# An encoder block in float32: the last normalization read from PSUM, residuals added two tiles at a time, and other first instructions

## The chip, the core and the metric

The kernel runs on one core of a Trainium2 chip. The core has five engines that run side by side, each from a queue of its own, strictly in order: TensorE (PE, matrix products; PEld is its weight load), VectorE (DVE), ScalarE (ACT), GpSimd (POOL) and SyncE (SP, which here only starts transfers). PE writes only to PSUM, eight banks of 128 x 512 float32; DVE and ACT read PSUM and SBUF; POOL works on SBUF alone. Transfers (DMA) go between HBM and SBUF and are started from the queues of SP, ACT and POOL.

The metric is the device time of one execution in microseconds (us).

## The reference: what is computed

One residual layer over 512 tokens of width 2048. The change touches its first product, its row sums of squares and its very last step, so these are shown; attention, convolution and gating lie between.

```python
def rms_norm(x, g):
    xf = x.astype(jnp.float32)
    y = xf * lax.rsqrt(jnp.mean(xf * xf, axis=-1, keepdims=True) + EPS) * g.astype(jnp.float32)
    return y.astype(x.dtype)
...
u = rms_norm(h, mix_pre_g[l])
proj = u @ w_in[l]
...
u = rms_norm(h, ffn_pre_g[l])
gate, up = jnp.split(u @ w_gate_up[l], 2, axis=-1)
f = (jax.nn.silu(gate) * up) @ w_down[l]
h = h + rms_norm(f, ffn_post_g[l])
```

## The kernel before

Everything is held transposed: 16 tiles of 128 features by 512 tokens (KT = 16). Tokens fall into halves `A` (columns 0 to 255) and `B` (256 to 511). A float32 product is made of three fast ones: each operand is split into a rounded part (`hi`, a cast on ACT, line 124) and the rest (`lo`, a subtraction on DVE, line 125), and PE adds hi·lo, hi·hi and lo·hi (lines 170, 173, 174 in `gemm`; 185, 187, 188 in `interleaved`). `wchunk` loads 1024 columns of weights from SP's queue and splits them.

A scheduler puts the instructions of each engine into one fixed order when the program is built, from program order and priorities; `keep_in_program_order` pins an instruction's place, and `high_priority(offset=-TAIL)` shifts the priority of what is inside by 200. At run time each engine takes its queue in that order and waits for semaphores at the head of it.

**The start** (lines 92 to 106 and 388 to 395). POOL makes an identity matrix, a tile of ones and `mhalf`, four columns of -0.5. PE runs WARM = 24 transposes of the identity, whose results nobody reads. ACT starts the transfers of `vec` (the gains) and of the second half of the first x tiles. `follow` pins the first ACT cast and the first product behind this. Then, for eight steps of two x tiles, ACT makes `u..h` (x times gain, line 137), DVE makes `u..l` (line 138), ACT squares x (line 325), DVE adds the squares up (line 328), and PE multiplies into four banks. The first weight chunk is split in two halves of 512 columns.

**A row's rms** (`rstd`, lines 277 to 295, and `by_column`). PE multiplies the tiles of squares by a column of ones: one 128x1 product per tile of squares and block of 128 tokens, into one column of a PSUM tile per block (`r.._s`). DVE scales that and adds EPS (line 292), POOL raises it to -0.5 (line 294), and PE spreads the result over 128 partitions (line 301, `r.._b`, in PSUM). For the last norm, `halves` has ACT copy that to SBUF (line 319, `r4`).

**The end** (lines 754 to 829). The w_down products run in two passes over the hidden dimension. In the second, DVE adds each result to `y` (line 772), ACT squares it, and ACT multiplies `y` by the post gain in place (line 774). The last two of the 16 features' tiles, 14 and 15, are computed by `products` for the token half A first and then for B, so that the work on half A's norm can lie beside the products of half B (`pl`, banks `pl1_14` and `pl1_15`). `first_half` then runs `finish` for 16 tiles of half A: y·r4 (line 794) and + h (line 795), on POOL for every third tile and on DVE otherwise, and SP starts one transfer out per tile (line 820). After the products of half B, DVE adds their results (line 786), ACT squares them (line 787), and the rms of half B, 16 more `finish` and five transfers out (line 829) end the kernel.

## Time and profile before

| | us |
|---|---|
| median of 3 runs (lowest, highest) | 2588.96 (2587.96, 2590.28) |
| the profiled execution | 2587.58 |
| its span, first to last instruction | 2585.8 |
| PE, DVE, ACT, POOL busy | 2535.4, 1751.2, 1079.6, 263.9 |
| mean granted TensorE clock | 0.991 of full |

The 1.8 us between the profiled execution's time and its span lie around the program. PE is busy for 98% of the span, so what can be saved lies in places where PE waits, and at the two ends, where the other engines work alone. Times in the rows below count from the span's start. In a group's row stand line, engine, operation, tiles written and read, the count, and then minimum, median and maximum of one instruction in nanoseconds or, in the rows by time, start and duration in us and the wait before it in brackets.

### The profile page before, as it was taken

The numbers are of one execution on the slowest core, as the hardware profiler recorded it, in microseconds if no ns is written. First come the engines' busy times: TensorE is split into PE (matmuls) and PEld (weight loads), VectorE is DVE, ScalarE is ACT, GpSimd is POOL, SyncE is SP. The second block draws the span as 40 slices with busy tenths as digits, with TensorE's granted clock in tenths as the row PEclk, the third lists the DMA queues.
The fourth block names the chain that finished last, engine by engine and source line by source line (L and its number), as shares of the span: only waits on it lengthen the run. The fifth ranks groups of instructions, "written<-read, shape, count | busy, mean of one in ns | idle before, by whom it ended". The sixth has DMA issues, their size and how long they took to land.

```text
span 2585.8 us, 33614 instructions
## 1 busy us (share of the span) xinstructions
PE 2535.4 (98%) x13078; PEld 2168.7 (84%) x13078; DVE 1751.2 (68%) x2224; ACT 1079.6 (42%) x1560; POOL 263.9 (10%) x290
## 2 busy tenths in 40 slices
PE   9999999989999999998999999999999999999996
PEld 8888888778888888887998888888888878888886
DVE  5999896687776655338888888888788832233336
ACT  5223333455554422224555555555555532233222
POOL 0110222320000011004100000000000100010003
PEclk9999999989999999999999999999999999999998
DMA  6234323356667435234356656656655653353334
GB/s 215 93 127 148 108 95 104 109 149 189 184 189 251 143 129 189 95 104 151 107 158 182 173 172 180 179 171 173 185 169 168 206 174 103 94 170 98 96 97 136
DMA packets 124624, 385.42 MB, mean 149 GB/s; under 512 B 14256, under 2 KB 21552, under 8 KB 124464
## 3 DMA queue, kind: packets, MB, share of 16 engines
q1 hardware_dynamic: 96464, 311.47, 37.0%
q0 software_dynamic: 13024, 45.62, 8.7%
q10 hardware_dynamic: 14976, 26.19, 2.8%
q8 instruction: 102, 1.67, 0.3%
q14 instruction: 58, 0.48, 0.1%
HBM read 350.72 MB, written 32.51 MB: 148 GB/s over the span
## 4 chain that ended last, share of the span: by engine, by line
PE 92%; DVE 4%; issue 2%; ACT 1%; DMA 1%; POOL 1%; POOLq 0%; DVEq 0%; ACTq 0%; SPq 0%
PE f L237 19%; PE f L239 10%; PE g L237 7%; PE pd L170 5%; PE pd L173 5%; PE pd L174 5%; PE g L239 3%; PE po L173 2%; PE po L174 2%; PE po L170 2%; PE qk L174 2%; PE qk L173 2%; PE qk L170 2%; PE py L170 2%; PE py L174 2%; PE py L173 2%
## 5 line engine op out<-in xcount | busy, mean ns | idle before, releaser
L125 DVE TENSOR_TENSOR wlo_wd<-raw_wd,whi_wd 128x1024 fp32r<-128x1024 f32 (+1 forms) x90 | 102.3, 1136 | 283.7 <-ACT whi_wd L124 283.7
L124 ACT CAST whi_wd<-raw_wd 128x1024 fp32r<-128x1024 f32 (+1 forms) x90 | 88.4, 982 | 312.8 <-PE pd L173 306.8
L376 DVE SCALAR_TENSOR_TENSOR cv<-z,vec,cv 128x497 f32<-128x497 f32 (+14 forms) x240 | 190.9, 797 | 4.7
L125 DVE TENSOR_TENSOR wlo_wo<-raw_wo,whi_wo 128x1024 fp32r<-128x1024 f32 x36 | 47.4, 1318 | 106.9 <-ACT whi_wo L124 106.9
L124 ACT CAST whi_wo<-raw_wo 128x1024 fp32r<-128x1024 f32 x36 | 37.9, 1054 | 130.0 <-PE po L173 122.7
L124 ACT CAST whi_y<-raw_y 128x1024 fp32r<-128x1024 f32 x32 | 33.5, 1052 | 78.8 <-PE py L173 75.5
L124 ACT CAST whi_qk<-raw_qk 128x1024 fp32r<-128x1024 f32 x32 | 33.6, 1051 | 77.1 <-PE qk L173 52.7
L125 DVE TENSOR_TENSOR wlo_qk<-raw_qk,whi_qk 128x1024 fp32r<-128x1024 f32 x32 | 40.4, 1261 | 32.3 <-ACT whi_qk L124 32.1
L125 DVE TENSOR_TENSOR wlo_y<-raw_y,whi_y 128x1024 fp32r<-128x1024 f32 x32 | 52.2, 1634 | 10.7 <-ACT whi_y L124 9.5
L616 DVE TENSOR_TENSOR gg<-py,gg 128x512 f32<-128x512 f32 x32 | 21.8, 690 | 53.1 <-PE py L174 53.1
L294 POOL TENSOR_TENSOR r_r<-r_v,mhalf 128x2 f32<-128x2 f32 (+1 forms) x6 | 7.7, 1283 | 458.2 <-DVE r_v L292 458.2
L735 POOL DMA_DIRECT2D ad<-a_d x44 | 24.0, 555 | 262.4 <-PE pd L170 197.6
L170 PE MATMUL py<-ycl,whi_y 128*128 128x512 f32 x128 | 49.8, 389 | 0.0
L173 PE MATMUL py<-ych,whi_y 128*128 128x512 f32 x128 | 49.8, 389 | 0.0
L174 PE MATMUL py<-ych,wlo_y 128*128 128x512 f32 x128 | 49.8, 389 | 0.0
L747 ACT ACTIVATE sg<-sg 128x512 f32<-128x512 f32 x39 | 24.7, 634 | 50.2 <-DVE sg L275 50.2
L455 POOL TENSOR_TENSOR bm<-braw,msk 128x128 f32<-128x128 f32 x56 | 43.0, 801 | 14.0 <-DMA braw<-in_rpb 13.9
L153 PE MATMUL f<-b,whi_f 128*128 128x256 f32 x128 | 36.2, 283 | 0.0
L154 PE MATMUL f<-b,wlo_f 128*128 128x256 f32 x128 | 36.2, 283 | 0.0
L152 PE MATMUL f<-b,whi_f 128*128 128x256 f32 x128 | 36.2, 283 | 0.0
L626 POOL TENSOR_TENSOR gg<-gg,gg 128x512 f32<-128x512 f32 x16 | 21.7, 1355 | 111.2 <-ACT whi_y L124 69.6
L124 ACT CAST whi_ca<-raw_ca 128x1024 fp32r<-128x1024 f32 x12 | 12.6, 1053 | 47.2 <-PE cb L173 19.0
(3045 smaller groups left out, 8284.4 us busy)
## 6 DMA issues: line engine op xcount, KB each, us to landing
raw_wd<-in_w_dn SPq DMA_DIRECT2D x60, 512.0 KB, 3.5
raw_wo<-in_w_out SPq DMA_DIRECT2D x36, 512.0 KB, 3.8
raw_qk<-in_w_qk SPq DMA_DIRECT2D x32, 512.0 KB, 3.7
raw_wd<-in_w_dn SPq DMA_DIRECT2D x30, 384.0 KB, 3.1
a_d<-sg ACTq DMA_DIRECT2D x44, 256.0 KB, 3.7
ad<-a_d POOLq DMA_DIRECT2D x44, 256.0 KB, 4.8
raw_v<-in_w_v SPq DMA_DIRECT2D x16, 512.0 KB, 4.4
raw_y<-in_w_ao SPq DMA_DIRECT2D x16, 512.0 KB, 3.7
```

What stands on the lines that cost most here:

```text
L124: nc.scalar.copy(hi[:, s], raw[:, s])
L125: nc.vector.tensor_tensor(out=lo[:, s], in0=raw[:, s], in1=hi[:, s].bitcast(F32), op=ALU.subtract)
L152: nc.tensor.matmul(o, hi, t[:, B], start=first, stop=False, skip_group_check=True)
L153: nc.tensor.matmul(o, hi, t[:, A], start=False, stop=False, skip_group_check=True)
L154: nc.tensor.matmul(o, lo, t[:, A], start=False, stop=last, skip_group_check=True)
L170: mmul = nc.tensor.matmul(ps, hi[:, s], al, start=first, stop=False)
L173: nc.tensor.matmul(ps, hi[:, s], ah, start=False, stop=False)
L174: nc.tensor.matmul(ps, lo[:, s], ah, start=False, stop=last)
L237: nc.tensor.matmul(ps, hi[:, ws[k]], t, start=first and k == 0, stop=False, skip_group_check=True)
L239: nc.tensor.matmul(ps[:, A], lo[:, ws[k]], t[:, A], start=False, stop=last and k == HT - 1, skip_group_check=True)
L376: nc.vector.scalar_tensor_tensor(out=a[:, to], in0=z[:, fr], scalar=col(C_WDW, i * CW + w), in1=a[:, to], op0=ALU.mult, op1=ALU.add)
L455: nc.gpsimd.tensor_tensor(out=bm[:, o + i - i0], in0=raw[:, :, i * BC : (i + 1) * BC], in1=msk[:, o + i - i0, None, :].broadcast_to([P, RO ...
```

## The change

- **Start.** `mhalf` is no longer set by POOL but computed by ACT from `ones`, pinned in its place: ACT's table load and this small instruction now stand ahead of the transfer of the second half of the first x tiles. The small `warm` instruction on ACT goes. PE's transposes become 17. The two halves of the first weight chunk are cast by DVE instead of ACT.
- **`rstd`** goes over the tiles of squares outside and over the token blocks inside, and only the very first product of a PSUM tile carries the start flag.
- **End.** The gain is no longer multiplied by ACT. `normalized` multiplies y by the gain and by 1/rms in one DVE instruction, which reads 1/rms straight from PSUM (`r.._b`); the copy `r4` goes. In half A the residual is added per tile, on DVE for every fourth tile and on POOL for twelve. In half B it is added for two tiles at once (128x512), on POOL for two of the eight pairs, and there are eight transfers out of two tiles each.

```diff
-WARM = 24
+WARM = 17
...
-    nc.gpsimd.memset(mhalf, -0.5)
-    warm = const.tile([P, 1], F32, name="warm")
-
+    tc.keep_in_program_order(nc.scalar.activation(mhalf, ones[:, :NB], AF.Copy, scale=-0.5))
     pw = abank("warm")
-    nc.scalar.activation(warm, mhalf[:, 0:1], AF.Square)
...
-    def wchunk(src, name, parts=1):
+    def wchunk(src, name, parts=1, cast=nc.scalar.copy):
...
-            nc.scalar.copy(hi[:, s], raw[:, s])
+            cast(hi[:, s], raw[:, s])
...
-        hi, lo = wchunk(w_c0[c], f"c0_{c}", 1 if c else 2)
+        hi, lo = wchunk(w_c0[c], f"c0_{c}", *((1,) if c else (2, nc.vector.tensor_copy)))
...
-        for t in blocks:
-            for i, a in enumerate(acc):
+        for i, a in enumerate(acc):
+            for t in blocks:
                 mmul = nc.tensor.matmul(
-                    ps[:, t : t + 1], a[:, t * P : (t + 1) * P], ones[:, 0:1], start=i == 0, stop=i == len(acc) - 1
+                    ps[:, t : t + 1], a[:, t * P : (t + 1) * P], ones[:, 0:1],
+                    start=i == 0 and t == blocks[0], stop=i == len(acc) - 1, skip_group_check=True,
                 )
...
-                    nc.scalar.activation(y[o], y[o], AF.Copy, scale=col(C_FPOST, o))
...
-    def finish(m, hm, cols, out):
-        e = nc.gpsimd if m % 3 == 2 else nc.vector
-        ym = y[m][:, cols]
-        e.tensor_tensor(out=ym, in0=ym, in1=r4[:, cols], op=ALU.mult)
-        e.tensor_tensor(out=out, in0=ym, in1=hm, op=ALU.add)
+    def normalized(out, m, cols):
+        nc.vector.scalar_tensor_tensor(
+            out=out, in0=y[m][:, cols], scalar=col(C_FPOST, m), in1=r4[0][:, cols], op0=ALU.mult, op1=ALU.mult
+        )
...
+    def halved(n, pin=False):
+        r = []
+        blocks = range(n * NB // 2, (n + 1) * NB // 2)
+        return (
+            lambda: r.append(rstd(acc + sq, D, f"r4{n}", blocks, pin)),
+            lambda: r4.insert(0, by_column(r[0], f"r4{n}", blocks, pin)),
+        )
...
             for m in range(KT):
-                finish(m, ha[m], A, y[m][:, A])
-                nc.sync.dma_start(ov[m, :, A], y[m][:, A])
+                ym = y[m][:, A]
+                normalized(ym, m, A)
+                e = nc.vector if m % 4 == 3 else nc.gpsimd
+                e.tensor_tensor(out=ym, in0=ym, in1=ha[m], op=ALU.add)
+                nc.sync.dma_start(ov[m, :, A], ym)
...
-    for i, k in ((0, 4), (4, 4), (8, 4), (12, 2), (14, 2)):
-        o = wp.tile([P, 4, HN], F32, tag="raw", name=f"o{i}", bufs=6)
-        for m in range(i, i + k):
-            finish(m, hb[m], B, o[:, m - i])
-        nc.sync.dma_start(ov[i : i + k, :, B].rearrange("k p t -> p k t"), o[:, :k])
+    for i in range(0, KT, 2):
+        o = wp.tile([P, 2, HN], F32, tag="raw", name=f"o{i}", bufs=6)
+        for m in range(2):
+            normalized(o[:, m], i + m, B)
+        e = nc.gpsimd if i % 8 == 0 else nc.vector
+        e.tensor_tensor(out=o, in0=o, in1=hb[i // 2], op=ALU.add)
+        nc.sync.dma_start(ov[i : i + 2, :, B].rearrange("k p t -> p k t"), o)
```

Between the start and the end the queues are the same as before, apart from the order of the 128x1 products of `rstd`. Three places show what moved.

ACT's queue at the start, before and after. `x` is the second half of the first x tiles, `whi_c_0` the rounded part of the first weight chunk.

```order
L93 DMA vec<-in_vecs 128x88
L347 DMA x_119<-in_xT 128x512
L137 ACT_TABLE_LOAD
L137 ACTIVATE u0h<-x_119,vec 128x512
L124 CAST whi_c_0_136<-raw_c_0_135 128x512
L325 ACTIVATE x_sq<-x_119 128x512
L137 ACTIVATE u1h<-x_119,vec 128x512
```

```order
L93 DMA vec<-in_vecs 128x88
L100 ACT_TABLE_LOAD
L100 ACTIVATE mhalf<-ones 128x4
L346 DMA x_110<-in_xT 128x512
L135 ACTIVATE u0h<-x_110,vec 128x512
L324 ACTIVATE x_sq<-x_110 128x512
L135 ACTIVATE u1h<-x_110,vec 128x512
```

The table load and `mhalf` moved ahead of the transfer, and the weight casts left this queue; on DVE each now stands directly ahead of `u0l` and `u1l`.

DVE's queue beside the products of half B, before: from the split of the next-to-last weight chunk (`wlo_wl1_0_16`) to that of the last (`wlo_wl1_1_16`), for which PE waits.

```order
L125 TENSOR_TENSOR wlo_wl1_0_16_21454<-raw_wl1_0_16_21452,whi_wl1_0_16_21453 128x768
L794 TENSOR_TENSOR y0_18449<-y0_18449,r4_21064 128x256
L794 TENSOR_TENSOR y1_18451<-y1_18451,r4_21064 128x256
L795 TENSOR_TENSOR y0_18449<-y0_18449,ha0_21065 128x256
L795 TENSOR_TENSOR y1_18451<-y1_18451,ha0_21065 128x256
L794 TENSOR_TENSOR y3_18625<-y3_18625,r4_21064 128x256
L794 TENSOR_TENSOR y4_18797<-y4_18797,r4_21064 128x256
L795 TENSOR_TENSOR y3_18625<-y3_18625,ha0_21065 128x256
L795 TENSOR_TENSOR y4_18797<-y4_18797,ha4_21067 128x256
L125 TENSOR_TENSOR wlo_wl1_1_16_21478<-raw_wl1_1_16_21476,whi_wl1_1_16_21477 128x768
```

The same piece of DVE's queue after the change.

```order
L789 SCALAR_TENSOR_TENSOR y0_18440<-y0_18440,vec_75,r40_b_21298 128x256
L123 TENSOR_TENSOR wlo_wl1_0_16_21427<-raw_wl1_0_16_21425,whi_wl1_0_16_21426 128x768
L789 SCALAR_TENSOR_TENSOR y1_18442<-y1_18442,vec_75,r40_b_21298 128x256
L789 SCALAR_TENSOR_TENSOR y2_18614<-y2_18614,vec_75,r40_b_21298 128x256
L789 SCALAR_TENSOR_TENSOR y3_18616<-y3_18616,vec_75,r40_b_21298 128x256
L789 SCALAR_TENSOR_TENSOR y4_18788<-y4_18788,vec_75,r40_b_21298 128x256
L827 TENSOR_TENSOR y3_18616<-y3_18616,ha0_21041 128x256
L789 SCALAR_TENSOR_TENSOR y5_18790<-y5_18790,vec_75,r40_b_21298 128x256
L123 TENSOR_TENSOR wlo_wl1_1_16_21451<-raw_wl1_1_16_21449,whi_wl1_1_16_21450 128x768
```

Eight instructions between the two splits became six, five of which read 1/rms from PSUM; one scale moved ahead of the first split. From the first split up to the sum of tile 15 (line 786 before, 784 after) stand 24 instructions before and 20 after.

PE's queue behind the last product of half B, before and after. `y_sq` is the sum of 14 tiles of squares, `sq_21062` and `sq_21039` are the squares of tile 14, `sq_21063` and `sq_21040` those of tile 15.

```order
L285 MATMUL r_s<-ones,y_sq 128x1
L285 MATMUL r_s<-ones,sq_21062 128x1
L285 MATMUL r_s<-ones,sq_21063 128x1
L285 MATMUL r_s<-ones,y_sq 128x1
L285 MATMUL r_s<-ones,sq_21062 128x1
L285 MATMUL r_s<-ones,sq_21063 128x1
```

```order
L283 MATMUL r_s<-ones,y_sq 128x1 x2
L283 MATMUL r_s<-ones,sq_21039 128x1 x2
L283 MATMUL r_s<-ones,sq_21040 128x1 x2
```

Of the six products, four stood from the first one on that needs tile 15's squares; now two do.

More of the change, by code (lines that the diff above doesn't have):

```diff
@@ L787, in products @@
             nc.scalar.activation(q[:, cols], y[o][:, cols], AF.Square)
-        for o in (KT - 2, KT - 1):
-            nc.scalar.activation(y[o][:, cols], y[o][:, cols], AF.Copy, scale=col(C_FPOST, o))
-    def finish(m, hm, cols, out):
-        e = nc.gpsimd if m % 3 == 2 else nc.vector
-        ym = y[m][:, cols]
-        e.tensor_tensor(out=ym, in0=ym, in1=r4[:, cols], op=ALU.mult)
-        e.tensor_tensor(out=out, in0=ym, in1=hm, op=ALU.add)
+    def normalized(out, m, cols):
+        nc.vector.scalar_tensor_tensor(
+            out=out, in0=y[m][:, cols], scalar=col(C_FPOST, m), in1=r4[0][:, cols], op0=ALU.mult, op1=ALU.mult
+        )
     ha = []
@@ L805, in hybrid_block @@
         ha += [t[:, 0], t[:, 1]]
+    def halved(n, pin=False):
[5 more added lines that the diff above has]
+        )
     products(0)
-    s1, s2 = halves(r4, acc + sq, "r4", 0, pin=True)
+    s1, s2 = halved(0, pin=True)
     hb = []
@@ L815, in first_half @@
             nc.sync.dma_start(t, h_d[i : i + 2, :, B].rearrange("k p t -> p k t"))
-            hb.extend((t[:, 0], t[:, 1]))
+            hb.append(t)
         with tc.high_priority(offset=-TAIL):
             for m in range(KT):
-                finish(m, ha[m], A, y[m][:, A])
-                nc.sync.dma_start(ov[m, :, A], y[m][:, A])
+                ym = y[m][:, A]
[3 more added lines that the diff above has]
+                nc.sync.dma_start(ov[m, :, A], ym)
     products(1, (s1, first_half))
-    for step in halves(r4, acc + sq, "r4", 1):
+    for step in halved(1):
         step()
-    for i, k in ((0, 4), (4, 4), (8, 4), (12, 2), (14, 2)):
-        o = wp.tile([P, 4, HN], F32, tag="raw", name=f"o{i}", bufs=6)
-        for m in range(i, i + k):
-            finish(m, hb[m], B, o[:, m - i])
-        nc.sync.dma_start(ov[i : i + k, :, B].rearrange("k p t -> p k t"), o[:, :k])
+    for i in range(0, KT, 2):
[5 more added lines that the diff above has]
+        nc.sync.dma_start(ov[i : i + 2, :, B].rearrange("k p t -> p k t"), o)
 def _mask():
```

2 lines of the change are left out of this document (1 added, 1 removed).

## The prediction

> **What bounds the kernel now.** I read the page first, then the chain that ended last over its final 40 us, then PE's instructions in order of time, then all engines in the first 10 us.
>
> ```profile
> PE 2535.4 (98%) x13078; PEld 2168.7 (84%) x13078; DVE 1751.2 (68%) x2224; ACT 1079.6 (42%) x1560; POOL 263.9 (10%) x290
> ```
>
> PE is the bound for nearly the whole span, and the queues between start and end stay as they were, so a gain or a loss can only lie where PE waits or has ended. The chain at the end (start, duration, what):
>
> ```profile
> 2548.23 0.96 DVE wlo_wl L125
> 2549.19 1.75 DVE y L794 x2
> ...
> 2556.22 1.40 DVE wlo_wl L125
> ...
> 2563.30 0.35 DVE y L786
> ...
> 2563.67 0.42 ACT sq L787
> ...
> 2564.14 1.88 PE r_s L285 x8
> ...
> 2566.28 0.72 POOL r_r L294
> ...
> 2567.04 1.24 PE r_b L301 x4
> ...
> 2568.30 0.38 ACT r L319
> ...
> 2581.13 0.42 DVE o L795
> ```
>
> From 2548 on the end hangs on DVE's queue, not on PE. PE's rows beside it:
>
> ```profile
> 2547.28 0.60 PE L301 MATMUL r_b<-ident,r_r 128*128 128x128 f32 x4
> ...
> 2557.67 0.39 PE L174 MATMUL pl<-fa38h,wlo_wl 128*128 128x256 f32 x1 [1.63 <-DVE wlo_wl L125]
> ...
> 2559.56 0.28 PE L174 MATMUL pl<-fa43h,wlo_wl 128*128 128x256 f32 x1
> ```
>
> PE stands still for 1.63 us because the last weight split comes late in DVE's queue; and when PE has ended (2559.84), tile 15's sum waits until 2563.30 behind half A's scales and adds.
>
> **Why DVE is late there.** Groups by line (minimum, median, maximum of one in ns):
>
> ```profile
> L794 DVE TENSOR_TENSOR y<-y,r x22: 411/422/957, 2549.1 to 2580.7; 128x256 f32<-128x256 f32 x22
> L794 POOL TENSOR_TENSOR y<-y,r x10: 897/906/1234, 2548.5 to 2574.0; 128x256 f32<-128x256 f32 x10
> L786 DVE TENSOR_TENSOR y<-pl,y x4: 417/422/425, 2538.2 to 2563.2; 128x256 f32<-128x256 f32 x4
> L668 DVE SCALAR_TENSOR_TENSOR u_0l<-f,vec,u_0h x2: 473/476/480, 1179.5 to 1185.7; 128x256 fp32r<-128x256 f32 x2
> ```
>
> A DVE operation on two SBUF tiles takes 0.41 us alone and up to 0.96 while POOL does the same. The new scale reads one tile from SBUF and one from PSUM. Whether POOL slows that too can be seen at 1243 us, where `f` lies in PSUM (first POOL's rows, then DVE's):
>
> ```profile
> 1243.45 1.29 POOL L697 TENSOR_TENSOR sg<-sg 128x512 f32<-128x512 f32 x1 [6.82 <-ACT sg L696]
> ...
> 1264.63 3.39 POOL L697 TENSOR_TENSOR sg<-sg 128x512 f32<-128x512 f32 x1 [17.48 <-ACT t L146]
> ```
>
> ```profile
> 1243.22 0.68 DVE L694 TENSOR_TENSOR sg<-f,r 128x512 f32<-128x512 f32 x1
> 1243.82 0.68 DVE L695 TENSOR_TENSOR sg<-f,r 128x512 f32<-128x512 f32 x1
> ...
> 1264.64 1.23 DVE L125 TENSOR_TENSOR wlo_f<-raw_f,whi_f 128x1024 fp32r<-128x1024 f32 x1
> ```
>
> Beside DVE operations with one PSUM input POOL's product took 1.29 us and they 0.68 each; beside a run of two-SBUF operations the same POOL product took 3.39. So the scales are priced at their undisturbed time.
>
> **Half A.** A scale lasts 0.476 us by L668. Neighbours on DVE overlap a little (L695 starts 0.60 after L694, which lasts 0.68), so a scale costs about 0.39 of the queue's time. `r_b` is in PSUM at 2547.88; the one scale now ahead of the first split runs in DVE's idle time and delays that split by 0.1 at most, which PE's earlier matmuls cover. From the end of the first split, 2549.19: 15 scales 5.9; three adds, each blocked by POOL as L794 is now, 3 x 0.9 = 2.7; the last split at its present disturbed 1.4; tile 14's sum 0.35. Tile 15's sum starts at 2559.5 instead of 2563.30: **-3.8**. Ends: adds at 0.34 and the split at 0.88 (its 0.96 less the overlap), both undisturbed, give 2557.3, and then PE decides at 2558.2, -5.1; scales at 0.48 give 2560.9, -2.4. The last split now stands behind four scales, an add and a scale: it starts at 2552.05 and ends by 2553.5, and PE wants it at 2557.67 - 1.63 = 2556.04. The stall goes, PE ends at 2558.2, and DVE is what is late next.
>
> POOL gets twelve adds here, ten operations before. At 0.9 each from 2548.4 they end at 2559.2, and the power for half B (L294) stands behind them in its queue. It is wanted at 2561.0, so 1.8 us are left. On SP the sixteen transfers out stay sixteen. The PSUM bank of half A's 1/rms is now held until tile 15's scale; half B's takes a bank that tile 14's sum has freed before, so that costs nothing.
>
> **The rms of half B.** Of six 128x1 products four stand from tile 15's squares on, 1.88 us; now two do, 0.94: **-0.9**. They run at half clock today, which the view by windows shows (length, PE busy, count, granted clock):
>
> ```profile
> 2558.00:2562.30 4.30, 1.96 (x18) 1.00 0.44 146
> 2562.40:2568.30 5.90, 3.61 (x14) 0.50 0.34 112
> ```
>
> The clock fell at 2562.3, when PE had been idle since 2559.84. With PE idle only from 2558.2 to 2560.3 I expect the two products at full clock, another **-0.4**; `r_b` too (0.60 at 2547.28 against 1.24) would be -0.6 more, which I leave to the range. The copy goes, 2568.30 to 2568.68: **-0.4**. ACT's multiplications by the gain leave its queue; nothing on this chain waits for them: 0. For the earlier norms the products only change places and PE has no wait on squares there: 0.
>
> **Half B's finish** takes 12.85 us now (2568.70 to 2581.55). After: 16 scales x 0.39 = 6.2; six DVE adds of 128x512 at 0.60, as L694 to L695; 0.3 for collisions with POOL's two adds: 10.1, **-2.7**. Ends: scales at 0.48 and both POOL adds blocking DVE for their whole 1.29 give 13.9, a loss of 1.0; no collision gives 9.8, -3.0. The eight transfers share six buffers:
>
> ```profile
> out<-o SPq DMA_DIRECT2D x2, 256.0 KB, 2.8
> ```
>
> The first pair is added on POOL by 2.1 us after the finish begins (two scales, 1.29) and out by about 5.3; the seventh pair wants its buffer after eleven scales and three adds, 6.1. No wait, with 0.8 in hand. The last pair's transfer has the size of today's last, so the 4.25 us from the last DVE operation to the span's end stay.
>
> [...]
>
> **The start.** Rows of the first 8 us, and two transfers (last number: us from issue to landing):
>
> ```profile
> 1.19 0.45 ACTq L347 DMA_DIRECT2D x<-in_xT  x1
> 1.46 4.90 PE L105 MATMUL warm<-ident 128*128 128x128 f32 x24 [1.46 <-POOL mhalf L99]
> 4.14 1.28 ACT L137 ACT_TABLE_LOAD   x1 [4.14 <-DMA x<-in_xT]
> 5.43 0.72 ACT L137 ACTIVATE u0h<-x,vec 128x512 fp32r<-128x512 f32 x1
> 6.86 0.69 DVE L125 TENSOR_TENSOR wlo_c<-raw_c,whi_c 128x512 fp32r<-128x512 f32 x1
> 7.60 0.50 PE L187 MATMUL c<-u0h,wlo_c 128*128 128x512 f32 x1 [0.38 <-DVE wlo_c L125]
> ```
>
> ```profile
> raw_c<-in_w_c SPq DMA_DIRECT2D x1, 256.0 KB, 4.0
> x<-in_xT ACTq DMA_DIRECT2D x1, 256.0 KB, 4.3
> ```
>
> The table load moves ahead of x's landing, so `u0h` can start 1.28 us earlier. Then the weights decide: issued at 1.18, landed at 5.2. The cast on DVE is not in the trace; between 0.42 (L786, half as long) and 0.69 (128x512, two inputs) I take 0.5. Cast 5.7, `u0l` 6.4, split 7.05: PE runs densely from 7.05 instead of 7.60. The second half of x is issued behind table load and `mhalf`, at 2.7 instead of 1.19, and lands at 7.0 by the same 4.3; cast, `u1l`, a sum and a split end at about 9.7, and PE wants them at 9.9. This leaves **-0.4** if the clock is up; the constant that POOL no longer writes lets the transposes begin at most 0.1 earlier.
>
> The warm-up decides that. Its records, and windows at other places:
>
> ```profile
> 2.70:5.70 3.00, 3.00 (x16) 1.00 0.94 329
> 5.70:6.40 0.70, 0.66 (x6) 1.00 1.00 383
> ```
>
> ```profile
> 521.14:524.55 3.41, 3.41 (x9) 0.50 0.74 247
> 524.55:527.97 3.42, 3.42 (x16) 1.00 0.52 165
> ```
>
> ```profile
> 541.62:545.03 3.41, 2.45 (x6) 0.50 0.54 169
> 545.03:548.45 3.42, 3.01 (x12) 0.50 0.98 269
> ```
>
> The transposes go 0.2 us apart until 5.7 and 0.12 after it, so PE starts slow and the clock rises there, though the column says 1.00 throughout. Elsewhere it changes at edges 3.41 apart; 3.01 busy in such a window raised it, 2.45 did not. Seventeen transposes keep PE busy from 1.46 to about 4.9. Over all places of the edges, 26% to 59% have a window with enough of that. Otherwise the clock rises between 9.3 and 11, and from 7.05 on products go at 9 per window instead of 16: 1.0 to 1.7 lost, **+0.5 to +1.2** in all. I take 0 between the two, with -0.6 and +1.2 as ends.
>
> **Sum.** -3.8 - 0.9 - 0.4 - 0.4 - 2.7 + 0 = -8.2 on the profiled execution's 2587.58, so 2579.4; that execution is 1.4 below the median of the runs, so **2580.8** as a median.
>
> **Rivals.** (1) POOL slows the PSUM scales too: at 0.88 as L794's pairs, half A gets 15 x 0.49 = 7.4 longer and half B about 1: +0.2, 2589. The rows at 1243 speak against it, though the operation there has another form. (2) Slower: POOL becomes the bound, the power waiting behind its twelve adds. An add may take 1.05 us for free; each 0.1 more costs 1.2; at 1.73 the gain is gone, at 2.2 it is 2594.6. For it speaks L697's 3.39 at twice the length, against it L794's 0.906 among 22 competing DVE operations, of which only four remain. (3) The clock rises late at the start in most executions: 2581.9. [...] (4) The change doesn't reach the end: the buffers of `o` come free late, each us one us, 2582 to 2583.
>
> **Chances.** The forecast with (3) and (4) inside it 0.87; (1) and other losses of half of the gain or more 0.09; (2) 0.04. Faster by over 0.2% (5.2 us, about what a measurement tells from no change) 0.85, within it 0.11, slower 0.04. The range: all best ends together (-5.1, -0.9, -1.0, -0.4, -3.0, -0.6) make -11.0, 2578.0, and I stop at 2578.2; scales at 0.48 (half A -2.4, half B 11.6 us, -1.2), the products at half clock and the start at +1.2 make -3.7, 2585.2, and I stop at 2585.0.
>
> **What the profile after would show.** Scales of half A at 0.42 to 0.48 us beside POOL's adds; no wait of PE's on the last split; tile 15's sum about 1 us behind PE's end; two products of tile 15's squares at full clock; DVE's first scale of half B about 5 us earlier than 2568.7, its last add about 8 us earlier than 2581.55; dense products from 7.0. Scales at 0.9, or the power starting late with DVE's rms value long ready, would make me wrong.

## The result

| | before | after |
|---|---|---|
| median of 5 runs, us (lowest, highest) | 2588.06 (2586.58, 2590.28) | 2576.27 (2573.37, 2577.51) |
| the profiled execution, its span | 2587.58, 2585.8 | 2577.34, 2575.5 |

The ratio is 0.9953 (95% interval 0.9941 to 0.9964): the change gains 11.8 us in the medians, where 8.2 were forecast. The sign was right; the median lies 1.9 below the forecast range. The spans of the two profiled executions are 10.3 apart.

**The profile after.** The engines' busy time on the page:

```profile
PE 2532.7 (98%) x13071; PEld 2166.2 (84%) x13071; DVE 1744.4 (68%) x2224; ACT 1065.8 (41%) x1538; POOL 258.6 (10%) x283
```

The chain that ended last, over the same stretch as before:

```profile
2549.83 1.53 DVE y L789 x4
2551.37 0.74 DVE y L827
...
2552.50 1.02 DVE wlo_wl L123
...
2554.70 0.67 DVE y L827
...
2557.27 0.37 DVE y L827
2557.64 1.06 DVE y L789 x3
2558.70 1.79 DMA out<-y
2560.54 0.71 POOL r_r L293
2561.30 0.72 PE r_b L300 x4
...
2562.44 1.33 DVE o L789 x4
...
2571.78 0.69 DVE o L839
```

It still begins on DVE. The transfer in it is a matter of hundredths: POOL's power starts 0.23 after DVE's rms value here, and 0.24 in the kernel before, where the chain names DVE. PE's rows by time:

```profile
2547.84 0.60 PE L300 MATMUL r_b<-ident,r_r 128*128 128x128 f32 x4
...
2556.43 0.28 PE L172 MATMUL pl<-fa38h,wlo_wl 128*128 128x256 f32 x1
...
2558.23 0.28 PE L172 MATMUL pl<-fa43h,wlo_wl 128*128 128x256 f32 x1
2558.36 0.50 PE L283 MATMUL r_s<-ones,y_sq 128*128 128x1 f32 x4
2558.72 0.58 PE L283 MATMUL r_s<-ones,sq 128*128 128x1 f32 x4
2559.65 0.61 PE L283 MATMUL r_s<-ones,sq 128*128 128x1 f32 x4 [0.35 <-ACT sq L785]
```

PE no longer waits for the last split (the row at 2556.43, the product that waited 1.63 before) and ends its products at 2558.51. DVE's rows behind it, first of the kernel before and then of the changed one (tile 15's sum, the rms value of half B, the first scale of half B):

```profile
2563.22 0.42 DVE L786 TENSOR_TENSOR y<-pl,y 128x256 f32<-128x256 f32 x1
2566.04 0.16 DVE L292 TENSOR_SCALAR r_v<-r_s 128x2 f32<-128x2 f32 x1 [2.40 <-PE r_s L285]
2568.70 0.42 DVE L794 TENSOR_TENSOR y<-y,r 128x256 f32<-128x256 f32 x1 [2.51 <-ACT r L319]
```

```profile
2558.74 0.41 DVE L784 TENSOR_TENSOR y<-pl,y 128x256 f32<-128x256 f32 x1
...
2560.30 0.16 DVE L291 TENSOR_SCALAR r_v<-r_s 128x2 f32<-128x2 f32 x1 [0.40 <-PE r_s L283]
2562.05 0.48 DVE L789 SCALAR_TENSOR_TENSOR o<-y,vec,r_b 128x256 f32<-128x256 f32 x1 [1.59 <-PE r_b L300]
```

These rows cut the end into five pieces, from the start of half A's `r_b` on PE (2547.28 before, 2547.84 after). DVE's last operation ends at 2581.55 before and 2572.47 after, and the last instruction of the span at 2585.81 and 2575.54.

| piece, us | before | after | difference | forecast |
|---|---|---|---|---|
| half A's `r_b` to tile 15's sum | 15.94 | 10.90 | -5.0 | -3.8 |
| to half B's rms value on DVE | 2.82 | 1.56 | -1.3 | -0.9 and -0.4 |
| to half B's first scale | 2.66 | 1.75 | -0.9 | -0.4 |
| half B's finish | 12.85 | 10.42 | -2.4 | -2.7 |
| DVE's last operation to the span's end | 4.25 | 3.07 | -1.2 | 0 |
| sum | 38.5 | 27.7 | -10.8 | -8.2 |

With the +0.6 that half A's `r_b` is late in this execution the pieces give the profiles' 10.3 but for rounding.

The groups of the end (minimum, median, maximum in ns):

```profile
L789 DVE SCALAR_TENSOR_TENSOR y<-y,vec,r_b x16: 468/471/479, 2548.5 to 2558.3; 128x256 f32<-128x256 f32 x16
L827 POOL TENSOR_TENSOR y<-y,ha x12: 723/738/1454, 2549.1 to 2558.9; 128x256 f32<-128x256 f32 x12
L827 DVE TENSOR_TENSOR y<-y,ha x4: 452/768/824, 2551.3 to 2559.1; 128x256 f32<-128x256 f32 x4
...
L839 DVE TENSOR_TENSOR o<-o,hb x6: 677/686/854, 2564.0 to 2571.8; 128x512 f32<-128x512 f32 x6
...
L839 POOL TENSOR_TENSOR o<-o,hb x2: 1264/1265/1266, 2563.1 to 2568.2; 128x512 f32<-128x512 f32 x2
```

Half A's sixteen scales keep within 11 ns of each other although POOL adds beside nearly all of them. DVE's own four adds, with two inputs in SBUF, take up to 824 ns, twice the 411 of L794 undisturbed. POOL's twelve adds take 0.738 in the median but 0.89 on the mean: two that meet DVE's weight splits took 1.32 and 1.45, three that meet DVE's own adds 0.92 to 0.93. The last of them ends at 2559.61.

**The start after**, on PE and on ACT:

```profile
7.00 0.79 PE L185 MATMUL c<-u0h,wlo_c 128*128 128x512 f32 x1 [0.41 <-DVE wlo_c L123]
7.60 0.63 PE L186 MATMUL c<-u0l,whi_c 128*128 128x512 f32 x1
...
10.14 0.39 PE L186 MATMUL c<-u0l,whi_c 128*128 128x512 f32 x1
```

```profile
1.19 1.28 ACT L100 ACT_TABLE_LOAD   x1 [1.19 <-PEq L913]
1.25 0.39 ACTq L346 DMA_DIRECT2D x<-in_xT  x1
```

The dense products begin at 7.00 as forecast, but 0.42 apart until 10.1, where they go 0.23 apart behind it: the late clock of the forecast's upper end. At the start the clock is read from this pace, half clock where it is near 0.42, since the column of the granted clock says 1.00 on both sides of 10.1.

### The profile page after: what moved, and what is told of

Its sections match the earlier page's. It is cut to its first block, busy times and chain, and to the rows that moved or that the text cites. A ratio compares the mean times of both kernels' runs of the same rounds, so it can differ in the third digit from the quotient of the medians.

```text
span 2575.5 us, 33581 instructions
## 1 busy us (share of the span) xinstructions
PE 2532.7 (98%) x13071; PEld 2166.2 (84%) x13071; DVE 1744.4 (68%) x2224; ACT 1065.8 (41%) x1538; POOL 258.6 (10%) x283
## 4 chain that ended last, share of the span: by engine, by line
PE 93%; DVE 3%; issue 1%; POOL 1%; DMA 1%; ACT 1%; SPq 0%; POOLq 0%; DVEq 0%; ACTq 0%
PE f L235 20%; PE f L237 10%; PE g L235 7%; PE pd L168 5%; PE pd L171 5%; PE pd L172 5%; PE g L237 4%; PE po L168 2%; PE po L171 2%; PE po L172 2%; PE qk L172 2%; PE qk L171 2%; PE qk L168 2%; PE py L168 2%; PE py L172 2%; PE py L171 2%
```

## The experiments

Two theories stood at first. One: the whole gain lies in the last 40 us, and the start gives nothing. Two: the part beyond the forecast comes from the start. All times are compared with runs of the kernel before made beside them. The pieces of the end, and where half A's `r_b` starts, come from one profiled execution each:

| kernel | half A's `r_b` at | to tile 15's sum | to rms value | to first scale | finish | to the end | sum |
|---|---|---|---|---|---|---|---|
| before | 2547.28 | 15.94 | 2.82 | 2.66 | 12.85 | 4.25 | 38.5 |
| after | 2547.84 | 10.90 | 1.56 | 1.75 | 10.42 | 3.07 | 27.7 |
| after, once more | 2545.15 | 10.90 | 1.56 | 1.75 | 10.43 | 3.07 | 27.7 |
| new end, old start | 2547.85 | 10.72 | 1.57 | 1.75 | 10.42 | 3.07 | 27.5 |
| after, 24 transposes | 2547.76 | 10.90 | 1.56 | 2.26 | 10.43 | 3.07 | 28.2 |
| after, 24, once more | 2548.61 | 10.90 | 1.55 | 2.26 | 10.43 | 3.07 | 28.2 |
| 1/rms copied to SBUF | 2544.95 | 16.20 | 1.96 | 2.66 | 12.17 | 3.07 | 36.1 |
| five adds on POOL | 2548.35 | 10.72 | 1.57 | 2.37 | 11.03 | 3.12 | 28.8 |
| squares by block | 2545.16 | 10.93 | 2.00 | 1.75 | 10.43 | 3.07 | 28.2 |
| five transfers | 2548.38 | 10.92 | 1.56 | 1.75 | 10.43 | 3.66 | 28.3 |
| single adds | 2543.60 | 10.89 | 1.56 | 1.75 | 11.00 | 3.09 | 28.3 |
| three pairs on POOL, 24 | 2548.62 | 10.91 | 1.55 | 1.75 | 9.99 | 3.07 | 27.3 |
| four pairs on POOL, 24 | 2545.07 | 10.91 | 1.56 | 1.75 | 9.91 | 3.65 | 27.8 |
| three pairs on POOL, 17 | 2547.09 | 10.91 | 1.55 | 1.99 | 9.99 | 3.08 | 27.5 |

### The end alone

```diff
-WARM = 17
+WARM = 24
...
-    tc.keep_in_program_order(nc.scalar.activation(mhalf, ones[:, :NB], AF.Copy, scale=-0.5))
+    nc.gpsimd.memset(mhalf, -0.5)
+    warm = const.tile([P, 1], F32, name="warm")
...
-        hi, lo = wchunk(w_c0[c], f"c0_{c}", *((1,) if c else (2, nc.vector.tensor_copy)))
+        hi, lo = wchunk(w_c0[c], f"c0_{c}", 1 if c else 2)
```

> The changed kernel with the start of the kernel before (24 transposes, the constant written by POOL, the first casts on ACT). Theory 1 (the whole gain is made in the last 40 us, the start gives 0): last 40 us as in the changed kernel (half A -5.1, row sums of half B -1.2, power to first scale -0.9, finish -2.4, span end -1.2), together -10.8; start as before, dense products from 7.6 with the clock up from 5.7; so 11 below the kernel before and within 0.5 of the changed kernel. Rival (the start gives the part that goes beyond the forecast): only 8 to 10 below the kernel before, and 1 to 3 above the changed kernel. Third reading, from the changed kernel's profile, whose clock rose late: the new start loses 0.8 there, so that this kernel is up to 1 us faster than the changed kernel.

2578.10 (2576.03 to 2578.46, 5 runs) against 2588.75 (15 runs): ratio 0.996, interval 0.9948 to 0.9973. The pieces are those of the changed kernel, and the runs' means differ by 10.5. So the end alone gives what its pieces say; the changed kernel's own median lies 1.8 lower still, in the rival's range.

### The start alone

The kernel before with the three parts of the new start:

```diff
-WARM = 24
+WARM = 17
...
-    nc.gpsimd.memset(mhalf, -0.5)
+    tc.keep_in_program_order(nc.scalar.activation(mhalf, ones[:, :NB], AF.Copy, scale=-0.5))
...
-        hi, lo = wchunk(w_c0[c], f"c0_{c}", 1 if c else 2)
+        hi, lo = wchunk(w_c0[c], f"c0_{c}", *((1,) if c else (2, nc.vector.tensor_copy)))
```

> The kernel before with the new start alone. Theory 1 (clock up in some executions, late in others): dense products from 7.05 instead of 7.60; -0.5 where the clock is up by 7, +0.8 where it rises at about 10, so the median between -0.5 and +1.2 of the kernel before. Rival (the new start gains in ways the profile does not show, such as an earlier second chunk): 1 to 3 below the kernel before. The last 40 us stay as before: 12.85 for half B's finish and 4.25 at the end.

2586.70 (11 runs) against the same 2588.75: ratio 0.9994, interval 0.9986 to 1.0003. The clock was up here (products 0.23 apart from 7.80 on) and the products of the third x tile began at 12.36 (12.94 before, 13.77 in the changed kernel's first profile). The medians differ by 2.1, which would be the rival's 1 to 3, the means by 1.55, with a standard error of 0.7: not settled by this run.

### 24 transposes in the changed kernel

```diff
-WARM = 17
+WARM = 24
```

> The changed kernel with 24 transposes instead of 17, so that PE is busy up to about 6.0 instead of 4.7. Theory 1 (a warm-up shorter than one clock window and a half seldom fills one window): the clock is up from 5 to 7, the products run at full clock from 7.0 on and the second step of the first projection is reached at 12.3 to 12.5 instead of 13.8; 0.6 to 1.5 faster than the changed kernel. Rival (the late clock was a chance of that one execution): same within 0.5, and the changed kernel's own new profiles show the clock up early.

The clock rose at 7.6 and the third tile's products began at 12.63, as expected, 1.1 earlier than in the changed kernel. Yet the median is 2577.77 (2575.51 to 2579.54), no faster than 2576.27, if anything slower. Theory 1 was right on the start and wrong on the time: what is gained by 14 us isn't there at 2547. The end shows the clock's other side; in this execution it had fallen before half B's 1/rms was spread:

```profile
2561.22 1.22 PE L300 MATMUL r_b<-ident,r_r 128*128 128x128 f32 x4 [1.04 <-POOL r_r L293]
```

1.22 in place of 0.71, and 2.26 in place of 1.75 to the first scale, with the same instructions. The kernel before had 1.24 at a granted clock of 0.50; in the changed kernel's 0.71 it was 1.00.

### 1/rms from SBUF instead of PSUM

```diff
+    r4s = slot("r4")
...
+    def into(pb, cols):
+        nc.scalar.copy(r4s[:, cols], pb[:, cols])
+        return r4s
...
-            lambda: r4.insert(0, by_column(r[0], f"r4{n}", blocks, pin)),
+            lambda: r4.insert(0, into(by_column(r[0], f"r4{n}", blocks, pin), (A, B)[n])),
```

> The changed kernel, but ACT copies each half's 1/rms to SBUF and the 32 scales read two SBUF tiles. Theory 1 (POOL and DVE hinder each other where DVE reads two SBUF tiles, and leave each other alone where one of them is in PSUM): beside POOL's adds half A's scales take 0.85 to 0.96 instead of 0.47, POOL's adds well over 0.74, the last split up to 1.4; tile 15's sum starts 3 to 6 later than 10.9 after half A's 1/rms; with the copies, 0.4 each, 4 to 7 slower than the changed kernel. Rival (the one-pass scale itself spares POOL, wherever it reads from): scales stay at 0.47, only the copies show, 0.4 to 0.8 slower. [...]

2584.09 (2582.24 to 2588.72, 10 runs), ratio 0.9986 (0.9977 to 0.9996): 7.8 slower than the changed kernel's 2576.27, and most of the gain is gone. Its groups:

```profile
L790 DVE SCALAR_TENSOR_TENSOR y<-y,vec,r x16: 472/939/961, 2546.8 to 2559.4; 128x256 f32<-128x256 f32 x16
L790 DVE SCALAR_TENSOR_TENSOR o<-y,vec,r x16: 471/476/1486, 2565.8 to 2576.7; 128x256 f32<-128x256 f32 x16
...
L832 POOL TENSOR_TENSOR y<-y,ha x12: 775/876/1320, 2547.4 to 2560.0; 128x256 f32<-128x256 f32 x12
...
L844 POOL TENSOR_TENSOR o<-o,hb x2: 1382/1382/1382, 2566.8 to 2572.8; 128x512 f32<-128x512 f32 x2
```

The same instruction takes 939 ns beside POOL when all it reads lies in SBUF, and 471 when 1/rms lies in PSUM. In half B POOL adds only twice, and one scale beside each of these adds takes 1.48 to 1.49 us, about as long as the add. Tile 15's sum comes 16.20 behind `r_b`, as late as in the kernel before; half B's finish takes 12.17. So it is the place of the operand that gives the gain, not the single pass; the rival is out. Theory 1 missed one size: the sum came 5.3 later, within its 3 to 6, but the finish's 1.75, half B's copy (0.4) and the clock that fell meanwhile (0.4 in the row sums, 0.5 in `r_b`) made 8.4 in the pieces where 4 to 7 were expected.

### Five of half A's adds on POOL

```diff
-                e = nc.vector if m % 4 == 3 else nc.gpsimd
+                e = nc.gpsimd if m % 3 == 2 else nc.vector
```

> The changed kernel with half A's residual adds dealt out as before: five on POOL, eleven on DVE. Theory 1 (DVE's queue sets tile 15's sum, and an add beside POOL costs 0.4 to 0.75): seven more adds ahead of it, less collisions with POOL; tile 15's sum 2.5 to 4.5 later than 10.9 after half A's 1/rms, the kernel as much slower. Rival (collisions with POOL's twelve adds cost as much as they save): within 0.5 of the changed kernel. Where PE decides (its last product ends 10.7 after half A's 1/rms) up to 0.2 of any lateness of DVE is free.

2579.12 (2574.64 to 2579.59, 4 runs), ratio 0.9958 (0.9942 to 0.9973). Theory 1 fell: tile 15's sum came no later but 0.2 earlier, at PE's end. Seven more adds on DVE did not count because they ran undisturbed (418 ns in the median), and because four scales and three adds of half A were put behind that sum, into the waits of half B's rms and into its finish:

```profile
L827 DVE TENSOR_TENSOR y<-y,ha x11: 413/418/460, 2550.3 to 2573.6; 128x256 f32<-128x256 f32 x11
L827 POOL TENSOR_TENSOR y<-y,ha x5: 722/740/798, 2551.6 to 2561.9; 128x256 f32<-128x256 f32 x5
```

DVE's last add of half A stands at 2573.63, behind half B's last: the finish grew to 11.03. What sets tile 15's sum in the changed kernel is PE and DVE at nearly the same time (2558.51 and 2558.74).

### The row sums by block again

```diff
-        for i, a in enumerate(acc):
-            for t in blocks:
+        for t in blocks:
+            for i, a in enumerate(acc):
...
-                    start=i == 0 and t == blocks[0], stop=i == len(acc) - 1, skip_group_check=True,
+                    start=i == 0, stop=i == len(acc) - 1, skip_group_check=True,
```

> The changed kernel with the row sums of squares by block again: for each block of 128 tokens all tiles of squares, a start flag for each block. Theory 1 (two more 128x1 products stand behind tile 15's squares): at full clock +0.3 to +0.5, at half clock +0.9, in the time from tile 15's sum to the 1/rms value on DVE (1.56 now); the kernel 0.3 to 0.9 slower, which lies below what its total time can tell, so the row decides. Rival (the products wait for nothing but each other): 1.56 stays.

```profile
2556.09 0.41 DVE L784 TENSOR_TENSOR y<-pl,y 128x256 f32<-128x256 f32 x1
...
2558.09 0.16 DVE L291 TENSOR_SCALAR r_v<-r_s 128x2 f32<-128x2 f32 x1 [0.85 <-PE r_s L283]
```

2.00 instead of 1.56: the order is worth 0.44 at full clock, within the 0.3 to 0.5 expected. The rest of the piece's -1.3 is the clock that is still up: the granted clock was 1.00 from 2558.50 to 2560.30 in the changed kernel, and 0.50 from 2562.40 on in the kernel before. The total, 2576.40 (2574.34 to 2580.90), cannot show it.

### Half B's transfers as before

```diff
-    for i in range(0, KT, 2):
-        o = wp.tile([P, 2, HN], F32, tag="raw", name=f"o{i}", bufs=6)
+    for i, k in ((0, 4), (4, 4), (8, 4), (12, 2), (14, 2)):
+        o = wp.tile([P, 4, HN], F32, tag="raw", name=f"o{i}", bufs=6)
```

> The changed kernel with half B's transfers out as before (4, 4, 4, 2 and 2 tiles, five in all), the residual still added by two tiles. The end of the span lay 4.25 behind DVE's last operation before and lies 3.03 behind it now, with a last transfer of the same 256 KB. Theory 1 (the last transfer waits behind 512 KB and 256 KB that were started just ahead of it): 3.8 to 4.3 again, finish unchanged at 10.4, the kernel 0.8 to 1.3 slower. Rival (before, SP was late and the two-input operation at the end was a different one; the sizes ahead don't matter): 3.0 to 3.2 stays.

From DVE's last operation to the end it takes 3.66, halfway between 3.07 and 4.25 and in neither theory's range; the finish stays at 10.43; the median is 2577.65 (4 runs). The view of transfers (number, size, median us from issue to landing), here and in the changed kernel:

```profile
out<-o SPq DMA_DIRECT2D x3, 512.0 KB, 3.0
out<-o SPq DMA_DIRECT2D x2, 256.0 KB, 2.6
```

```profile
out<-o SPq DMA_DIRECT2D x8, 256.0 KB, 2.2
```

The last transfer alone lands after 2.5 here, 2.1 in the changed kernel and 2.8 before. So the grouping of the transfers counts for about half of the 1.2: 0.4 in the landing, and 0.2 between the landing and the span's end (0.90 in the changed kernel, 1.09 here and 1.10 before). Of the other half, 0.35 is that SP started the last transfer of the kernel before only at 2581.93, though DVE's last operation had ended at 2581.55; in the changed kernel 0.03 lie between the two. What held it no row names. The rest is the landing of 2.8 against 2.5 here, which stays open.

### One add of two tiles, or two adds

```diff
-        e.tensor_tensor(out=o, in0=o, in1=hb[i // 2], op=ALU.add)
+        for m in range(2):
+            e.tensor_tensor(out=o[:, m], in0=o[:, m], in1=hb[i // 2][:, m], op=ALU.add)
```

> The changed kernel with half B's residual added tile by tile (two 128x256 instructions in place of one 128x512), on the same engines, with the same transfers. Theory 1 (a 128x512 add occupies DVE for 0.60, two of 128x256 for 2 x 0.34): six pairs x 0.08 = +0.5 on DVE; on POOL 2 x 0.74 for 1.27, collisions +0.1 to +0.3; finish 10.9 to 11.2 instead of 10.42. Rival (the gain of the finish lies in adding two tiles at once): 11.5 or more.

A finish of 11.00, as theory 1 has it: adding by two tiles brings 0.6 of the finish's 2.4, and 1.75 is the PSUM operand (above). The one run took 2573.69, less than most runs of the changed kernel although its end is 0.6 longer: half A's `r_b` started at 2543.60 in it.

### More of half B's adds on POOL

Both with 24 transposes. Pairs 0, 4 and 8 on POOL instead of 0 and 8; then pairs 0, 4, 8 and 12 (the line below), with the last two tiles added and sent out one by one.

```diff
-        e = nc.gpsimd if i % 8 == 0 else nc.vector
+        e = nc.gpsimd if i % 4 == 0 else nc.vector
```

> The changed kernel with 24 transposes and with three instead of two of half B's adds on POOL (pairs 0, 4 and 8 of the eight two-tile steps, by their first tile). Theory 1 (DVE's queue sets the finish): one add of 0.60 less on DVE, a collision of up to 0.3 more, finish 10.0 instead of 10.4; with the start, 1 to 2 faster than the changed kernel. Rival (POOL slows DVE by what it takes over, or a buffer comes free late since three transfers now wait for POOL): finish 10.4 to 11, no gain over the 24 transposes alone.

> The changed kernel with 24 transposes, four of half B's adds on POOL (pairs 0, 4, 8 and 12 by their first tile) and the last two tiles added on DVE and sent out one by one. Three adds of POOL's gave a finish of 9.99 instead of 10.42. Theory 1 (each pair moved to POOL takes 0.60 off DVE and costs about 0.17 in collisions; a last transfer of half the size lands earlier): finish 9.5 to 9.8, from DVE's last operation to the span's end 2.7 instead of 3.05; together 1.0 to 1.3 less than the changed kernel in these rows, though its total may hide that. Rival (POOL's fourth add is itself late and the transfers queue behind it): finish 10.0 or more, or an end above 3.1.

Three pairs: finish 9.99 as expected; but the median, 2577.67 (2575.51 to 2578.14), is not the expected 1 to 2 below the changed kernel's, and the ratio, 0.9958, can't be told from the 0.9961 of 24 transposes alone. Four pairs: finish 9.91, above the 9.5 to 9.8 expected, and 3.65 to the end: the rival's late transfers. POOL's last pair is started out at 2568.61 and the last two tiles only at 2569.07 and 2569.58, 0.38 behind DVE's end. 2576.93 (2574.63 to 2579.22), ratio 0.9961 (0.9948 to 0.9975): no better.

### Is there a gain in the start after all?

By now kernels with 24 transposes lay above those with 17 by more than their ends. The changed kernel ran once more; then came the new start alone again, the kernel before with 17 transposes as its only edit, the kernel before with the new start but 24 transposes, and the changed kernel with 24 again. Their edits are those shown above: the new start with or without its line of `WARM`, or that line alone.

> The changed kernel as it is, on the chip and in the rounds of the candidate. Theory 1 (the last 40 us give the gain, the middle differs by up to 5 us between executions of the same instructions): from half A's 1/rms to tile 15's sum 10.7 to 10.9 and a finish of 10.4 again, 10 to 12 below the kernel before; the clock at the start up at about 10, or before 7 in some executions, without a trace of it in the total. Rival (the gain beyond the last 40 us' 10.8 is real and comes from the start): 11.5 or more below the kernel before, with dense products from 7.0 at full clock.

> The kernel before with the new start alone, once more (it gave 0.9994 of the kernel before, interval 0.9986 to 1.0003). Theory 1 (the new start brings about 1.2 through the middle): 1.0 to 2.0 below the kernel before on the mean. Rival (spread of the middle, which differs by up to 5 us between executions of the same instructions): within 0.7 of it.

> The kernel before with 17 transposes instead of 24, nothing else. Theory 1 (it is the number of transposes that counts): 1.0 to 2.0 below the kernel before on the mean, although the dense products start no earlier than 7.6. Rival (the order on ACT and the casts on DVE count, or nothing does): within 0.7 of it, or up to 1 above where the clock rises late.

> The kernel before with the new start but 24 transposes. Theory 1 (the 17 transposes bring the 1.2): 0 to 0.6 below the kernel before on the mean, since the clock is up and the dense products start 0.5 earlier. Rival (the other parts of the start bring it): 1.0 to 2.0 below.

> The changed kernel with 24 transposes, once more. Theory 1: 10.3 to 11.0 below the kernel before on the mean, as the tail alone gives. Rival (spread): anywhere from 10 to 12.5, with the changed kernel's own mean (12.5 below) inside the spread of this one.

| kernel | runs | mean less the mean of the kernel before | standard error | ratio and interval |
|---|---|---|---|---|
| new start alone | 11 | -1.55 | 0.71 | 0.9994 (0.9986, 1.0003) |
| new start alone, again | 11 | -2.16 | 0.55 | 0.9991 (0.9982, 1.0000) |
| 17 transposes alone | 11 | -0.11 | 0.65 | 0.9998 (0.9990, 1.0007) |
| new start, 24 transposes | 11 | -0.13 | 0.50 | 0.9998 (0.9989, 1.0007) |
| whole change | 5 | -12.47 | 0.99 | 0.9953 (0.9941, 0.9964) |
| whole change, again | 5 | -12.14 | 1.05 | 0.9953 (0.9940, 0.9965) |
| whole change, 24 | 5 | -10.27 | 0.86 | 0.9961 (0.9948, 0.9975) |
| whole change, 24, again | 5 | -10.49 | 0.97 | 0.9958 (0.9945, 0.9970) |
| end alone | 5 | -10.54 | 0.68 | 0.9960 (0.9948, 0.9973) |
| squares by block | 5 | -10.96 | 1.33 | 0.9956 (0.9941, 0.9970) |
| five transfers | 4 | -10.45 | 0.88 | 0.9956 (0.9941, 0.9971) |
| 1/rms copied to SBUF | 10 | -3.61 | 0.85 | 0.9986 (0.9977, 0.9996) |
| five adds on POOL | 4 | -9.92 | 1.30 | 0.9958 (0.9942, 0.9973) |
| three pairs on POOL, 24 | 5 | -11.10 | 0.75 | 0.9958 (0.9945, 0.9970) |
| four pairs on POOL, 24 | 5 | -10.46 | 1.14 | 0.9961 (0.9948, 0.9975) |

The whole start lies 2.16 below, a little more than the 1.0 to 2.0 of theory 1. Its parts bring nothing alone: 17 transposes -0.11, as their rival has it, the rest -0.13. Together they lie 1.9 below on the mean (22 runs, standard error 0.4), but the interval of each ratio reaches 1, so a gain of the start is likely and not shown. The changed kernel, run again, lies 12.1 below, more than the 10 to 12 of its theory 1; its rival has the number, but not the cause, since the products ran at half clock from 7.6 to 11.0.

In the whole change 17 transposes are 1.9 ahead of 24 (ten runs each, standard error 1.0). 0.5 of that lies in the end: in both profiles with 24 half B's `r_b` runs at half clock. The other kernels with the new end point the same way, less strongly. Set against what their own pieces of the end give, the seven with 17 transposes and more than one run lie 0.2 to 2.4 lower, 1.1 on the mean of their 38 runs (the version of the last experiment below among them); the five with 24 lie between 0.5 higher and 0.2 lower.

And whatever it is, it isn't made at the start: the repeat of the start alone reached the third tile at 14.28, 1.3 later than the kernel before, and half A's `r_b` 1.1 earlier. Set side by side row by row, executions of the same instructions part at five places, mostly by 1 to 3 us each and once by 4.3: near 520 to 550, 810, 830, 870 and 1200 to 1240, where PE waits or the clock falls for 3.4 us or more. One of them can be followed. At 810 PE waits for a copy on ACT that stands behind a cast, and the cast waits for a transfer of the attention result. In the changed kernel with 24 transposes (ACT, PE, and the three transfers' time from issue to landing):

```profile
808.94 0.62 ACT L132 CAST ya1h<-ar 128x512 fp32r<-128x512 f32 x1 [2.63 <-DMA ar<-att_d]
```

```profile
810.10 2.12 PE L235 MATMUL g<-t,g15h 128*128 128x512 f32 x8 [1.13 <-ACT g15v L225]
```

```profile
DMA to landing us min/median/max: 4.3/6.1/6.3
```

and in the changed kernel, where PE does not wait there:

```profile
809.31 0.62 ACT L132 CAST ya1h<-ar 128x512 fp32r<-128x512 f32 x1 [1.30 <-DMA ar<-att_d]
```

```profile
DMA to landing us min/median/max: 4.4/4.7/5.0
```

The middle value is 4.7 to 5.2 in all eleven profiles with 17 transposes and 5.1 to 6.6 in all seven with 24; PE waits at 810 in none of the eleven, and for 0.2 to 1.7 in each of the seven. Why seven transposes at the start should move a transfer at 803 is open; nothing here shows it. Nor is it shown to be the gain: the kernel before with 17 transposes alone has the early landing too (4.9, no wait of PE's) and gained nothing.

### The version that is left

The changed kernel, 17 transposes, with pairs 0, 4 and 8 of half B on POOL.

```diff
-        e = nc.gpsimd if i % 8 == 0 else nc.vector
+        e = nc.gpsimd if i in (0, 4, 8) else nc.vector
```

> The changed kernel with three of half B's adds on POOL (pairs 0, 4 and 8), and 17 transposes as changed. Theory 1 (the start's gain depends on its 17 transposes, the finish on DVE's queue): finish 9.99 and 3.07 behind it, the transfer of the attention result at 810 landing 4.7 to 5.2 after its start, and on the mean 12 to 13 below the kernel before, 0.4 less than the changed kernel. Rival (the difference between 17 and 24 transposes was chance): 10.5 to 11.5 below the kernel before, as with 24.

2574.85 (2572.77 to 2576.39, 5 runs) against 2588.10: ratio 0.9947 (0.9934 to 0.9961), 13.4 by the means (standard error 0.7), a little more than the 12 to 13 of theory 1 and well beyond the rival's 11.5. Its finish:

```profile
2561.54 0.48 DVE L789 SCALAR_TENSOR_TENSOR o<-y,vec,r_b 128x256 f32<-128x256 f32 x1 [1.82 <-PE r_b L300]
```

```profile
2570.84 0.69 DVE L839 TENSOR_TENSOR o<-o,hb 128x512 f32<-128x512 f32 x1
```

9.99 from the one to the end of the other, and 4.9 for the transfer at 810. It is ahead of the kernel before beyond doubt, and of the changed kernel by the 0.43 of its finish, which the totals can't tell.

## Why the prediction was right and where it was wrong

The gain was 3.6 larger than forecast (11.8 against 8.2, in medians). 2.6 of this lies in the pieces of the end: half A was priced too dear (1.2), the end of the span was put at no change (1.2), and `r_b` at full clock was left out of the sum (0.5), while the finish brought 0.3 less. These are the steps that failed, and the mechanism behind them was right in half A and wrong at the span's end. The other 1.0 does not lie in the end; it may come from the start, and that is not settled. Besides, the forecast counted from 2588.96, the median of three runs; that of five is 2588.06.

**Right: where the time is, and the sign.** The gain at the end is in the places named: no PE wait on the last split, two products of tile 15's squares at full clock, one copy less, a shorter finish. The price on which most hung, scales undisturbed at 0.476 beside POOL, was measured at 0.471, and the version that copies 1/rms to SBUF shows that this is the mechanism: 0.939 there. Nor did the PSUM source cost anything in itself: 468 ns at least from PSUM, 471 and 472 from SBUF. POOL's twelve adds took 0.89 on the mean, the 0.9 assumed, and its power started 0.07 behind the end of DVE's value, so rivals 1 and 2 are out; no buffer of `o` was late (4). Rival 3, the late clock, came in the first profile and cost there what was forecast (0.8 at the third x tile), but the runs' times don't carry it.

**Half A, -3.8 against -5.0: a size.** The step "three adds, each blocked by POOL as L794 is now, 3 x 0.9 = 2.7; the last split at its present disturbed 1.4" was too dear: the adds took 0.74, 0.67 and 0.37 of the chain, the split 1.02, together 1.3 less. Both were priced by rows in which nearly every DVE operation competes with POOL. The forecast's own best end, -5.1 with PE deciding, nearly came: DVE reaches the sum 0.23 behind PE's end.

**The rms of half B, -1.3 each: right.** The order alone gives 0.44 at full clock (twice that, the forecast's 0.9, at half clock), the clock the rest. `r_b` at full clock, left to the range as -0.6 more, came in this profile (0.72 in the chain, 1.24 before) and in 8 of the 13 profiles of changed ends tabled above; with the copy's -0.4 it makes the -0.9.

**Half B's finish, -2.7 against -2.4: nearly.** The scales are as priced. Two of the adds meet POOL and take 0.85, and before five of the six the chain has 0.22 to 0.25 for which it names no cause and which the forecast did not count. Single adds gave 11.00.

**"The 4.25 us from the last DVE operation to the span's end stay": wrong, -1.2.** The argument looked only at the last transfer's size. With eight even transfers fewer bytes are in flight when it starts (256 KB, issued at 2571.38 and landed 2.1 later, against 512 KB and 256 KB in the kernel before, issued at 2579.51 and 2580.79 and landed 3.2 and 2.9 later), and it lands sooner, after 2.1 instead of 2.8: half of the 1.2 goes with the grouping, by the run with the old one. Of the other half, 0.35 is SP's late start in the kernel before, whose cause is open, like the rest.

**The start, 0 against -1.9 on the means, not settled: the forecast's reach was too short.** The step was right in its rows (dense from 7.00; clock late in some executions) and took one thing wrong: the second half of x was not issued "behind table load and `mhalf`, at 2.7" but at 1.25. What failed is to stop at 14 us. 0.6 earlier or 0.8 later there does not arrive at 2547; what arrives is decided at a few places far behind. On the means this start came out 1.9 ahead with the end as before and about 1 ahead with the new ends; why is open, and no row of the trace before could have priced it.

Put together, -5.0 - 1.3 - 0.9 - 2.4 - 1.2 at the end and -1.9 of the start would make -12.7; the ten runs of the changed kernel lie 12.1 and 12.5 below the kernel before by their means. The forecast's range ended at -10.8, about the end alone.

## What to carry to other kernels

Where VectorE and GpSimd work side by side, look at where the inputs lie: with one PSUM operand DVE's scales took 471 ns here beside POOL's adds and these 738, both in the median, and copying that operand to SBUF first made it 939 and 876 and took back 8 us. Price an operation from rows with the competition it will have, not with what it has now, and follow the end of a kernel to the last landing, since the transfers ahead of the last one are part of it (3.66 with five transfers here, 3.07 with eight). A gain at the start of a long kernel is not a gain at its end until runs show it: profile rows there are exact to hundredths, and executions of the same instructions came apart by 5 us further on.

## What the runs showed of the hardware

- A transfer in ACT's queue was started at 1.25 while ACT's table load ran from 1.19 to 2.47: the load ahead of it did not hold it.
- With two SBUF inputs DVE's scale doubled beside POOL (471 to 939 ns), while POOL's add only went from 738 to 876 in the median: the two did not pay alike.
- The clock at the start, by the pace of the transposes and products (products 0.23 us apart where it is up, 0.43 where it is not), rose between 4.3 and 10.9 us, at another time in almost every profile; in the repeat of the start alone it rose at 5.03, fell at 8.45 and rose at 11.86, edges 3.41 us apart. At the end it fell between 2558.2 and 2565.0, in some executions before half B's `r_b` (1.22 us for it) and in others after it (0.72). At the start it was up by 7.8 with 24 transposes and stayed up in each of seven profiles; with 17 it did so in five of eleven, fell again for 3.4 us at about 8 in four and rose only after 10 in two.
- Half A's `r_b` started anywhere between 2543.6 and 2548.6 in eighteen profiles of kernels whose instructions between 40 and 2540 us are the same but for the order of some 128x1 products.
